# An attention kernel with bias: seven wide warm-up products for fourteen, the first two bias slots in a row, and the late k transposes behind score slot 2

## Chip, cores and metric

The kernel runs on one core of a Trainium2 chip. The metric is device time in microseconds (us) of one execution; lower is better. A timed run is mostly some 1.8 us longer than its span, because the span covers only the first to the last recorded instruction. Single runs of one kernel scatter by up to a microsecond, so that differences below 0.5 us need several runs each.

TensorE is PE in the views (its weight loads PEld), VectorE is DVE, ScalarE is ACT, GpSimd is POOL and SyncE is SP. PEq, SPq and ACTq are the queues of these engines. The columns of a timeline: start in us, duration in us, engine, line, operation, out<-in, count.

## The reference

```python
# batch 4, 8 heads, 1024 positions, 64 numbers per head; bias is 1 x 1 x 1024 x 1024
scores = (1.0 / np.sqrt(head_dim)) * np.matmul(q, k.transpose(0, 1, 3, 2)) + bias
scores_max = np.max(scores, axis=-1, keepdims=True)
attn = np.exp(scores - scores_max) / (np.sum(np.exp(scores - scores_max), axis=-1, keepdims=True) + 1e-8)
return np.matmul(attn, v).astype(np.float32)
```

## The kernel before

The kernel takes heads in 16 pairs. A score slot is up to three 128 x 512 products of k and q in PSUM; ACT exponentiates it (`s_exp`). exp(score + bias) is made as exp(score) times exp(bias), so the bias is exponentiated once, in four bias slots of 16 transposes and one ACT instruction each (`b_fill`, `b_exp`), and DVE multiplies it in. Two PSUM buffers (`ps_s`) serve score and bias slots in turn. After a hand-written opening, a small greedy scheduler, run when the program is built, puts the rest in order from estimated costs.

```python
    raws = {}
    trs = {}

    def load_qk(pr):
        qr = raw.tile([P, 2, NCH, D], BF, name="qr")
        kr = raw.tile([P, 2, NCH, D], BF, name="kr")
        nc.gpsimd.dma_start(out=kr.rearrange("p t c d -> p t (c d)"), in_=kf[pr])
        nc.gpsimd.dma_start(out=qr.rearrange("p t c d -> p t (c d)"), in_=qf[pr])
        raws[pr] = (qr, kr)
# ... cut ...
    def s_fill(g):
        if ("S", g) not in open_ps:
            open_ps[("S", g)] = ps_s.tile([P, 3, HQ], F32, tag="s", name="ps")
        ps = open_ps[("S", g)]
        for j, b in enumerate(slots[g]):
            pr, h, qh, kc = banks[b]
            qT, kT = trs[(pr, 0)], trs[(pr, 1)]
            nc.tensor.matmul(ps[:, j, :], kT[:, kc, :], qT[:, h, qh * HQ:(qh + 1) * HQ],
                             start=True, stop=b not in late_bias)
# ... cut ...
    def s_exp(g):
        n = len(slots[g])
        nc.scalar.activation(e_at(slots[g][0], n), open_ps.pop(("S", g))[:, :n, :], ACTF.Exp, scale=scale)

    def b_fill(qh, c0):

        ps = ps_s.tile([P, 3, 2 * HQ], BF, tag="s", name="pb").rearrange("p b (k c q) -> p (b k) c q", c=2, q=P)
        open_ps[("B", qh, c0)] = ps
        for c in range(2):
            for kc in range(NCH):
                nc.tensor.transpose(ps[:, kc, c, :],
                                    btraw[:, qh * QC + c0 + c, :].rearrange("p (kp kc) -> p kc kp", kc=NCH)[:, kc, :],
                                    ident[:])

    def b_exp(qh, c0):
        nc.scalar.activation(eb[:, qh, :, c0 * P:(c0 + 2) * P],
                             open_ps.pop(("B", qh, c0))[:, :NCH].rearrange("p k c q -> p k (c q)"), ACTF.Exp)
# ... cut: multiplication by exp(bias), products with v, division ...
        def evac():
            oh = small.tile([P, M, D], F32, name=f"oh{x}")
            rs = small.tile([P, M, 1], F32, name=f"rh{x}")
            nc.vector.reciprocal(rs[:], acc[:, :, D:D1])
            q = (nc.scalar, nc.sync)[x]
            if x == 0:
                for i in range(M):
                    nc.scalar.activation(oh[:, i, :], acc[:, i, :D], ACTF.Copy, scale=rs[:, i, :])
            else:
                nc.vector.tensor_tensor(oh[:], acc[:, :, :D], rs[:].to_broadcast([P, M, D]), op=ALU.mult)
            q.dma_start(out=of[2 * NP - 1][:, QC + x * M:QC + (x + 1) * M, :], in_=oh[:])
        return evac      # the last two stores of the kernel
```

The opening, which the change edits:

```python
        nc.gpsimd.dma_start(out=kr0[:, :, QC:, :].rearrange("p t c d -> p t (c d)"), in_=kf[0][:, :, QC * D:])
        nc.gpsimd.dma_start(out=btraw[:, :2, :], in_=bf_[:, :2, :])
        nc.gpsimd.dma_start(out=qr0[:, :, QC:, :].rearrange("p t c d -> p t (c d)"), in_=qf[0][:, :, QC * D:])
        nc.gpsimd.dma_start(out=btraw[:, 2:QC, :], in_=bf_[:, 2:QC, :])
        for x in range(2):
            for y in range(2):
                nc.vector.memset(mask[x * D:(x + 1) * D, y, :], 1.0 if x == y else 0.0)

        wm = ps_s.tile([P, 3, HQ], F32, tag="s", name="ps")
        open_ps[("S", 0)] = wm

        def dummy(n):
            nc.tensor.matmul(wm[:, 0, :n], zeros[:, :P], zeros[:, :n], start=True, stop=True)

        for i in range(12):
            dummy(HQ // 2)

        def k_trans(c0, n, tag):
            px = ps_x.tile([P, n, P], BF, tag=tag, name="px")
            for c in range(n):
                for t in range(2):
                    nc.tensor.transpose(px[t * D:(t + 1) * D, c, :], kr0[:, t, c0 + c, :], ident[:])
            return px
# ... cut: q_trans, q_out, first casts and copies ...
        q_out(1, pq1)
        nc.scalar.copy(kr0[:, :, 2:QC, :], k0f[:, :, 2:, :])
        dummy(P)
        dummy(P)
        s_fill(0)
        s_exp(0)
        s_fill(1)
        pk1 = k_trans(2, 2, "xa")
        nc.vector.tensor_copy(kT0[:, 2:QC, :], pk1[:])
        nc.vector.memset(vall[:, :, :, D:D1], 1.0)
        s_exp(1)
        pk2 = k_trans(QC, QC, "xb")
        s_fill(2)
        nc.vector.tensor_copy(kT0[:, QC:, :], pk2[:])
        s_exp(2)
        load_v(0)
        for c in (QC, QC + 2):
            nc.gpsimd.dma_start(out=btraw[:, c:c + 2, :], in_=bf_[:, c:c + 2, :])
        load_qk(1)
        load_v(1)
        load_qk(2)
        EXP, EXP0, QK, AV, TP = 427, 62, 216, 170, 350
        MUL, COPYQ, COPYK, EVAC, SEM = 600, 650, 420, 620, 80
        order = [("S", g) for g in range(3, NS)]
        for at, x in ((3, (0, 0)), (5, (0, 2)), (9, (1, 0)), (11, (1, 2))):
            order.insert(at, ("B",) + x)
        NO = len(order)
        T0 = 8000.0
        t_act, t_pe, t_dve = T0 + 1400, T0 + 200, T0 + 100
        filled = []
# ... cut: the scheduler ...
```

The softmax here doesn't subtract the row's maximum and nothing guards it: scores larger than these inputs give would overflow.

Of the kernel before, what the change touches and what calls it, by code (L numbers as in the profile page):

```python
# [9 lines left out]
BF = mybir.dt.bfloat16  # L10
# [5 lines left out]
def kernel(  # L16
# [15 lines left out]
    nc = tc.nc  # L32
    B, H, S, D = q.shape
    P = 128
# [4 lines left out]
    HQ = S // 2  # L39
    QC = NCH // 2  # L40
# [7 lines left out]
    consts = ctx.enter_context(tc.tile_pool(name="consts", bufs=1))  # L48
# [15 lines left out]

    k0f = consts.tile([P, 2, QC, D], F32)
    q0f = [consts.tile([P, QC, D], F32, name=f"q0f{t}") for t in range(2)]
    zeros = consts.tile([P, HQ // 2], BF)

    raws = {}
    trs = {}  # L70
# [8 lines left out]
    def load_v(pr):  # L79
        for t in range(2):  # L80
            nc.gpsimd.dma_start(out=vall[:, 2 * pr + t, :, :D], in_=vf[pr, :, t])  # L81
# [34 lines left out]
    def e_at(b, n):  # L116
        if b // ET not in etiles:
            etiles[b // ET] = ep.tile([P, ET, HQ], BF, name="E")
        return etiles[b // ET][:, b % ET:b % ET + n, :]
# [3 lines left out]
# [9 lines that stand above are left out]
            if b in late_bias:  # L132
                nc.tensor.matmul(ps[:, j, :], ident[:], braw[:, late_bias[b], :], start=False, stop=True)
# [4 lines that stand above are left out]
# [105 lines left out]
    with tc.manual_schedule():  # L243
# [12 lines left out]
        kT0 = kvp.tile([P, NCH, P], BF, name="kT")  # L256
# [13 lines left out]
        wm = ps_s.tile([P, 3, HQ], F32, tag="s", name="ps")  # L270
        open_ps[("S", 0)] = wm

        def dummy(n):
            nc.tensor.matmul(wm[:, 0, :n], zeros[:, :P], zeros[:, :n], start=True, stop=True)  # L274

        for i in range(12):
            dummy(HQ // 2)

        def k_trans(c0, n, tag):
            px = ps_x.tile([P, n, P], BF, tag=tag, name="px")  # L280
# [4 lines that stand above are left out]
# [18 lines left out]
            "p b (c q) -> p (b c) q", q=P)[:, :QC, :])  # L303
        q_out(1, pq1)
        nc.scalar.copy(kr0[:, :, 2:QC, :], k0f[:, :, 2:, :])
        dummy(P)
        dummy(P)
        s_fill(0)
        s_exp(0)
        s_fill(1)  # L310
# [1 line left out]
        nc.vector.tensor_copy(kT0[:, 2:QC, :], pk1[:])  # L312
        nc.vector.memset(vall[:, :, :, D:D1], 1.0)
        s_exp(1)
        pk2 = k_trans(QC, QC, "xb")
        s_fill(2)
        nc.vector.tensor_copy(kT0[:, QC:, :], pk2[:])  # L317
        s_exp(2)
        load_v(0)
        for c in (QC, QC + 2):  # L320
            nc.gpsimd.dma_start(out=btraw[:, c:c + 2, :], in_=bf_[:, c:c + 2, :])  # L321
# [7 lines left out]
        EXP, EXP0, QK, AV, TP = 427, 62, 216, 170, 350  # L329
        MUL, COPYQ, COPYK, EVAC, SEM = 600, 650, 420, 620, 80  # L330
        order = [("S", g) for g in range(3, NS)]
        for at, x in ((3, (0, 0)), (5, (0, 2)), (9, (1, 0)), (11, (1, 2))):
            order.insert(at, ("B",) + x)
        NO = len(order)
        T0 = 8000.0
        t_act, t_pe, t_dve = T0 + 1400, T0 + 200, T0 + 100
        filled = []
        act_end = []
        x_free = {"xa": T0 - 500, "xb": T0 + 100}
        x_unit = {}  # L340
        bias_at = {(0, 0): 10900, (0, 2): 13700, (1, 0): 18600, (1, 2): 20800}
        raw_at = {0: (5900, 11500), 1: (22200, 23500), 2: (26000, 28500)}
        pieces = [(0, 0, 1)]
        for pr in range(1, NP):
            pieces += [(pr, 1, 0), (pr, 0, 0), (pr, 1, 1), (pr, 0, 1)]

        pieces.append((NP, 0, 0))
        raw_at[NP] = (T0, T0)
        piece_end = {(0, 1, 0): T0, (0, 0, 0): T0, (0, 1, 1): T0 + 200}
        eb_at = {}  # L350
        exp_at = {x: T0 + (0 if x < 3 else 1400) for x in range(6)}
        mul_at = {}
# [16 lines left out]
        def pe_cost(t, c):  # L369
            return c * 2 if t < COLD else c  # L370
# [207 lines left out]
        while len(act_end) < NO or av_next < NA or any(last_left) or dve_q:  # L578
# [12 lines left out]
            if who == 0:  # L591
                i = a[2]
                item = order[i]
                t_act = t + a[1]
# [12 lines left out]
            elif who == 1:  # L607
                if d in dve_q:
                    dve_q.remove(d)
                t_dve = t + d[2]  # L610
                d[3](t)
            else:
                t_pe = t + pe_cost(t, p[1])
# [31 lines left out]
```

## Time and profile before

| | before |
|---|---|
| device time, median of 3 (lowest to highest) | 249.80 us (249.74 to 250.32) |
| span of the profiled run | 249.0 us |
| ACT busy | 240.1 us, 96% |
| start of the unbroken run of 161 exponentials | 27.53 us |
| its 161 exponentials | 215.95 us |
| start of ACT's last store issue | 244.87 us |
| from there to the end of the span | 4.13 us |

The span of this kernel can be read as three stretches, which I shall call **front**, **middle** and **tail**. The front ends where ACT's unbroken run begins. The middle reaches from there to the start of ACT's last store issue: 244.87 - 27.53 = 217.34 us. The tail is the rest: 249.0 - 244.87 = 4.13 us. It holds the landing of the last two stores and the closing of the program.

The page has the whole span's count of these blocks:

```profile
q8 instruction: 25, 0.41, 0.7%
```

0.41 MB / 25 is some 16 KB each. The Trainium skill's page "Runtime: NRT & Kernel Launch", section "Instruction fetch mechanics", says that an engine's instruction memory is refilled in blocks of 16 KiB, 256 instructions, by the engine's own DMA queue while it executes, and that the cost of crossing a block boundary is "mostly hidden". The size agrees, and 25 x 256 = 6400 is near the 6354 instructions of PE in the built program (DVE, the next, has 419), so I take q8 for PE's.

### The profile page before, as it was taken

What the parts mean: (1) busy time and instruction counts of PE and PEld (TensorE: products, weight loads), DVE (VectorE), ACT (ScalarE), POOL (GpSimd) and SP (SyncE); (2) the same over time, 40 slices, a digit from 0 to 9 for tenths busy, and PEclk for the clock granted to TensorE, in tenths of its full rate; (3) what the DMA queues carried; (4) which work ended last, traced back from release to release, by engine and by line L of the source; (5) the groups of instructions that cost most, each with busy time, mean ns of one, the idle gap of its engine ahead of it and who ended that gap; (6) DMA issues with size and microseconds to landing.
All of it is one profiled execution on the core that took longest, in us unless ns stands there. A gap on an engine that the chain in (4) does not pass through costs nothing.

```text
span 249.0 us, 7149 instructions
## 1 busy us (share of the span) xinstructions
PE 226.3 (91%) x3106; PEld 141.6 (57%) x3160; DVE 219.0 (88%) x381; ACT 240.1 (96%) x183; POOL 54.6 (22%) x76
## 2 busy tenths in 40 slices
PE   8768999999999999999999999999999999998892
PEld 4335656556665665665656555666555555565561
DVE  5207899999999999999999999999998999999883
ACT  5999999999999999999999999999999999999991
POOL 6654534202213501303230041416000000000000
PEclk9999999999999999999999999999999999999999
DMA  5999999923925994922992049789901101020201
GB/s 118 176 199 192 202 135 197 98 84 45 147 56 100 135 81 121 90 88 29 180 133 84 5 95 118 94 124 122 131 3 42 46 23 65 3 84 3 87 32 57
DMA packets 48752, 23.80 MB, mean 96 GB/s; under 512 B 34512, under 2 KB 44624, under 8 KB 48720
## 3 DMA queue, kind: packets, MB, share of 16 engines
q0 software_dynamic: 42560, 14.42, 53.5%
q1 hardware_dynamic: 5872, 8.72, 9.7%
q8 instruction: 25, 0.41, 0.7%
q10 hardware_dynamic: 288, 0.20, 0.3%
q14 instruction: 7, 0.06, 0.1%
HBM read 29.36 MB, written 8.39 MB: 152 GB/s over the span
## 4 chain that ended last, share of the span: by engine, by line
ACT 65%; PE 18%; DVE 7%; DMA 5%; issue 2%; POOL 1%; ACTq 0%
ACT E L137 64%; PE ps L130 11%; DMA kr<-in_k_dram 5%; PE po L188 3%; DVE E L163 2%; PE px L89 2%; PE ps L274 1%; DVE E L160 1%; DVE E L157 1%; DVE oall L200 1%; DVE qT L98 1%; ACT eb L150 1%; POOL vall L81 1%; POOL btraw L321 0%; PE pb L145 0%
## 5 line engine op out<-in xcount | busy, mean ns | idle before, releaser
L137 ACT ACTIVATE E<-ps 128x1536 bf16<-128x1536 f32 (+2 forms) x172 | 230.1, 1666 | 0.7 <-PE ps L130 0.7
L130 PE MATMUL ps<-qT,kT 128*128 128x512 bf16 x458 | 134.8, 379 | 12.1 <-ACT E L137 5.6
L188 PEld LDWEIGHTS <-E 128*128 128x128 bf16 x2016 | 82.0, 98 | 40.2 <-DVE E L160 3.8
L160 DVE TENSOR_TENSOR E<-E,eb 128x2048 bf16<-128x2048 bf16 x78 | 93.9, 1216 | 5.9 <-ACT eb L150 5.7
L188 PE MATMUL po<-vall,E 128*128 128x65 bf16 x2016 | 92.7, 194 | 2.5 <-DVE E L160 1.3
L130 PEld LDWEIGHTS <-kT 128*128 128x128 bf16 x512 | 45.1, 97 | 41.6 <-issue 9.9
L163 DVE TENSOR_TENSOR E<-E,eb 128x1024 bf16<-128x1024 bf16 x92 | 61.1, 684 | 1.9 <-ACT E L137 1.4
L75 POOL DMA_DIRECT2D kr<-in_k_dram x15 | 10.5, 699 | 87.1 <-PE px L89 84.1
L81 POOL DMA_DIRECT2D vall<-in_v_dram x32 | 28.1, 883 | 4.8 <-DVE kT L317 3.5
L200 DVE TENSOR_TENSOR oall<-po,rs 128x256 f32<-128x256 f32 x63 | 26.7, 425 | 2.2
L98 DVE TENSOR_TENSOR qT<-px,mask 128x1024 bf16<-128x1024 bf16 x31 | 21.3, 688 | 6.7 <-PE px L89 6.0
L76 POOL DMA_DIRECT2D qr<-in_q_dram x15 | 10.7, 715 | 26.0 <-PE px L89 22.8
L102 DVE COPY kT<-px 128x512 bf16<-128x512 bf16 x30 | 12.6, 421 | 1.9 <-PE px L89 1.5
L198 DVE RECIPROCAL rs<-po 128x4 f32<-128x4 f32 x63 | 11.1, 177 | 2.4 <-PE po L188 2.2
L89 PE MATMUL px<-ident,kr 128*64 128x128 bf16 x240 | 12.4, 224 | 0.8 <-DMA kr<-in_k_dram 0.6
L89 PE MATMUL px<-ident,qr 128*64 128x128 bf16 x248 | 12.8, 225 | 0.1
L89 PEld LDWEIGHTS <-qr 128*64 128x64 bf16 x248 | 7.9, 109 | 8.0 <-issue 5.1
L89 PEld LDWEIGHTS <-kr 128*64 128x64 bf16 x240 | 7.7, 109 | 7.6 <-issue 4.5
L150 ACT ACTIVATE eb<-pb 128x2048 bf16<-128x2048 bf16 x4 | 7.5, 1883 | 0.4 <-PE pb L145 0.4
L145 PE MATMUL pb<-ident,btraw 128*128 128x128 bf16 x64 | 4.6, 225 | 1.2 <-ACT eb L150 1.0
L145 PEld LDWEIGHTS <-btraw 128*128 128x128 bf16 x64 | 4.4, 146 | 1.5 <-issue 1.1
L157 DVE TENSOR_TENSOR E<-E,eb 128x1024 bf16<-128x1024 bf16 (+2 forms) x7 | 4.6, 686 | 0.2 <-ACT E L137 0.2
(45 smaller groups left out, 28.2 us busy)
## 6 DMA issues: line engine op xcount, KB each, us to landing
out_dram<-oall SPq DMA_DIRECT2D x28, 256.0 KB, 2.0
vall<-in_v_dram POOLq DMA_DIRECT2D x32, 128.0 KB, 5.9
kr<-in_k_dram POOLq DMA_DIRECT2D x15, 256.0 KB, 4.5
qr<-in_q_dram POOLq DMA_DIRECT2D x15, 256.0 KB, 5.2
btraw<-in_bias_dram POOLq DMA_DIRECT2D x4, 512.0 KB, 8.5
out_dram<-oall SPq DMA_DIRECT2D x7, 128.0 KB, 3.5
k0f<-in_k_dram SPq DMA_DIRECT2D x2, 128.0 KB, 3.0
q0f<-in_q_dram ACTq DMA_DIRECT2D x1, 128.0 KB, 2.5
```

The source lines that it names most:

```text
L76: nc.gpsimd.dma_start(out=qr.rearrange("p t c d -> p t (c d)"), in_=qf[pr])
L81: nc.gpsimd.dma_start(out=vall[:, 2 * pr + t, :, :D], in_=vf[pr, :, t])
L89: nc.tensor.transpose(px[t * D:(t + 1) * D, c, :], src[:, t, half * QC + c, :], ident[:])
L98: nc.vector.tensor_tensor(dst[:, :, half * HQ:(half + 1) * HQ], px.rearrange("p c q -> p (c q)").unsqueeze(1).to_broadcast([P, 2, HQ]), ma ...
L102: nc.vector.tensor_copy(dst[:, half * QC:(half + 1) * QC, :], px[:])
L130: nc.tensor.matmul(ps[:, j, :], kT[:, kc, :], qT[:, h, qh * HQ:(qh + 1) * HQ], start=True, stop=b not in late_bias)
L137: nc.scalar.activation(e_at(slots[g][0], n), open_ps.pop(("S", g))[:, :n, :], ACTF.Exp, scale=scale)
L160: nc.vector.tensor_tensor(e, e, eb[:, qh, kc:kc + 2, :].unsqueeze(2).to_broadcast([P, 2, 2, HQ]), op=ALU.mult)
L163: nc.vector.tensor_tensor(e, e, eb[:, qh, kc:kc + 1, :].to_broadcast([P, n, HQ]), op=ALU.mult)
L188: nc.tensor.matmul(acc[:, i, :], e[:, 0, i * P:(i + 1) * P], vall[:, 2 * pr + h, kc, :], start=(kc == 0 and i == 0), stop=(kc == NCH - 1), ...
L198: nc.vector.reciprocal(rs[:], acc[:, :, D:D1])
L200: nc.vector.tensor_tensor(oall[:, c0:c0 + QC, :], acc[:, :, :D], rs[:].to_broadcast([P, QC, D]), op=ALU.mult)
```

## The change

The intent is a cheaper opening. (1) TensorE is warmed by seven dummy products of the same total width in place of fourteen, over a smaller tile of zeros. (2) The eight late k transposes leave the path to score slot 2. (3) The first two bias slots are taken in a row, ahead of the transposes of the second half of q, so that exp(bias) for the first half of the queries is ready sooner. The other edits are the scheduler's estimates for the new order.

```diff
--- before.py
+++ after.py
@@ -64,7 +64,7 @@
 
     k0f = consts.tile([P, 2, QC, D], F32)
     q0f = [consts.tile([P, QC, D], F32, name=f"q0f{t}") for t in range(2)]
-    zeros = consts.tile([P, HQ // 2], BF)
+    zeros = consts.tile([P, P], BF)
 
     raws = {}
     trs = {}
@@ -271,10 +271,11 @@
         open_ps[("S", 0)] = wm
 
         def dummy(n):
-            nc.tensor.matmul(wm[:, 0, :n], zeros[:, :P], zeros[:, :n], start=True, stop=True)
-
-        for i in range(12):
-            dummy(HQ // 2)
+            nc.tensor.matmul(wm[:, 0, :n * P], zeros[:, :P], zeros[:, :P].unsqueeze(1).to_broadcast([P, n, P]),
+                             start=True, stop=True)
+
+        for i in range(6):
+            dummy(QC)
 
         def k_trans(c0, n, tag):
             px = ps_x.tile([P, n, P], BF, tag=tag, name="px")
@@ -303,8 +304,7 @@
             "p b (c q) -> p (b c) q", q=P)[:, :QC, :])
         q_out(1, pq1)
         nc.scalar.copy(kr0[:, :, 2:QC, :], k0f[:, :, 2:, :])
-        dummy(P)
-        dummy(P)
+        dummy(2)
         s_fill(0)
         s_exp(0)
         s_fill(1)
@@ -312,10 +312,11 @@
         nc.vector.tensor_copy(kT0[:, 2:QC, :], pk1[:])
         nc.vector.memset(vall[:, :, :, D:D1], 1.0)
         s_exp(1)
+        s_fill(2)
+        s_exp(2)
         pk2 = k_trans(QC, QC, "xb")
-        s_fill(2)
-        nc.vector.tensor_copy(kT0[:, QC:, :], pk2[:])
-        s_exp(2)
+        nc.vector.tensor_copy(kT0[:, QC:QC + 1, :], pk2[:, :1, :])
+        nc.vector.tensor_copy(kT0[:, QC + 1:, :], pk2[:, 1:, :])
         load_v(0)
         for c in (QC, QC + 2):
             nc.gpsimd.dma_start(out=btraw[:, c:c + 2, :], in_=bf_[:, c:c + 2, :])
@@ -329,24 +330,24 @@
         EXP, EXP0, QK, AV, TP = 427, 62, 216, 170, 350
         MUL, COPYQ, COPYK, EVAC, SEM = 600, 650, 420, 620, 80
         order = [("S", g) for g in range(3, NS)]
-        for at, x in ((3, (0, 0)), (5, (0, 2)), (9, (1, 0)), (11, (1, 2))):
+        for at, x in ((3, (0, 0)), (4, (0, 2)), (9, (1, 0)), (11, (1, 2))):
             order.insert(at, ("B",) + x)
         NO = len(order)
         T0 = 8000.0
-        t_act, t_pe, t_dve = T0 + 1400, T0 + 200, T0 + 100
+        t_act, t_pe, t_dve = T0 + 1400, T0 + 200, T0 + 600
         filled = []
         act_end = []
-        x_free = {"xa": T0 - 500, "xb": T0 + 100}
+        x_free = {"xa": T0 - 500, "xb": T0 + 600}
         x_unit = {}
         bias_at = {(0, 0): 10900, (0, 2): 13700, (1, 0): 18600, (1, 2): 20800}
-        raw_at = {0: (5900, 11500), 1: (22200, 23500), 2: (26000, 28500)}
+        raw_at = {0: (5900, 14300), 1: (22200, 23500), 2: (26000, 28500)}
         pieces = [(0, 0, 1)]
         for pr in range(1, NP):
             pieces += [(pr, 1, 0), (pr, 0, 0), (pr, 1, 1), (pr, 0, 1)]
 
         pieces.append((NP, 0, 0))
         raw_at[NP] = (T0, T0)
-        piece_end = {(0, 1, 0): T0, (0, 0, 0): T0, (0, 1, 1): T0 + 200}
+        piece_end = {(0, 1, 0): T0, (0, 0, 0): T0, (0, 1, 1): T0 + 500}
         eb_at = {}
         exp_at = {x: T0 + (0 if x < 3 else 1400) for x in range(6)}
         mul_at = {}
```

## The prediction

> **What bounds the kernel now.** I read the page first (busy shares), then the waits of ScalarE (ACT), then ACT's timeline, and last the chain of waits of the first 30 us, because every part of the change sits in the first 28 us. The page's first section and the waits of ACT:
>
> ```profile
> PE 226.3 (91%) x3106; PEld 141.6 (57%) x3160; DVE 219.0 (88%) x381; ACT 240.1 (96%) x183; POOL 54.6 (22%) x76
> ```
>
> ```profile
> ACT oh L237 <- DVE rh L233: 0.8, 1, 0.8
> ACT E L137 <- PE ps L130: 0.7, 3, 0.2
> ...
> ACT eb L150 <- PE pb L145: 0.4, 1, 0.4
> ```
>
> ACT computes 172 exponentials of scores (L137) and 4 of the bias (L150) and is busy 240.1 of 249.0 us. After the first score exponential starts (5.71 us) it waits only 0.23 + 0.25 + 0.21 us ahead of its first three exponentials, 0.36 us ahead of the fourth bias slot, and 0.84 us in the tail. ACT's timeline:
>
> ```profile
> 23.94 1.45 ACT L137 ACTIVATE E<-ps 128x1536 bf16<-128x1536 f32 x1
> 25.75 1.88 ACT L150 ACTIVATE eb<-pb 128x2048 bf16<-128x2048 bf16 x1 [0.36 <-PE pb L145]
> 27.53 215.95 ACT L137 ACTIVATE E<-ps 128x1536 bf16<-128x1536 f32 x161
> ```
>
> From 27.53 to 243.48 us ACT never stops: 161 exponentials, 215.95/161 = 1.341 us each. The change alters no size or number there, so the end moves by as much as the start of that unbroken run moves, which is set by the fourth bias exponential at 25.75. What released that one? The chain of waits, first 30 us (start, us, what):
>
> ```profile
> 8.53 1.75 POOL vall L81 x2
> 10.28 1.06 POOL btraw L321 x2
> 11.34 11.35 DMA kr<-in_k_dram
> 22.69 0.04 issue
> 22.73 0.41 PE px L89 x8
> ...
> 24.72 1.01 PE pb L145 x16
> 25.73 0.02 issue
> 25.75 1.88 ACT eb L150
> 27.63 2.69 ACT E L137 x2
> ```
>
> So the path does not come from ACT's early work. It comes from the load of the next pair's k, issued at 11.34 and landed at 22.69. TensorE (PE), in order, stands at the 8 transposes that need it; then come one score slot (3 matmuls), some AV matmuls (scores times v), 8 q transposes and the 16 bias transposes, and only then can ACT go on. ACT had run without a gap from 7.78 until here.
>
> **What the Trainium skill says.** "TensorE: Matmul & The Clock Gate", section "Back-to-back issue gap", gives N/1.2 ns from matmul to matmul while cold. The 12 dummies of 256 columns took 2.74 us with 0.421 us for one: (2.74 - 0.421)/11 = 0.211 us, and 256/1.2 = 0.213. The trace agrees. The same page, "What's actually happening", has the clock go full after a busy window of about 3.4 us that is free-running. In the trace a 512-column matmul takes 0.61 us at 5.06 us and 0.39 us at 6.90, so the switch lies between; whether it is free-running one trace can't show. "ScalarE: Activation LUTs", section "What ACT_TABLE_LOAD costs", gives 186 ns + 0.833 ns per element with 93 ns of overlap: 1.373 us a step for 1536 elements, where the trace has 1.341; I use the trace. "Perfetto Trace Analysis", section "Per-instruction lifecycle", says that the slice of a DMA issued by GpSimd ends when the descriptors are written, not when data has moved. The trace agrees: the k load's slice is 0.71 us, its landing 11.35 us after the issue.
>
> **The change part by part.**
>
> (1) Dummies. Twelve of 256 columns become six of 512; two of 128 become one of 256. Columns before: 12 x 256 + 2 x 128 = 3328; after: 6 x 512 + 256 = 3328. Cold spacing goes with columns, so PE is busy equally long: 11 x 0.211 + 0.421 = 2.74 us before; after, 5 x 0.422 + 0.61 = 2.72 us. The memset of the zeros is halved, 0.17 us to some 0.1 (an estimate by size), so they may start 0.07 us earlier. The first transposes wait for q anyway: its cast ends at 3.28 + 0.29 = 3.57. Worth 0 to 0.07 us at the first exponential.
>
> (2) Eight late k transposes behind score slot 2. Before, they stand ahead of slot 2: 8 of about 0.04 us, 0.3 us. Slot 2's second matmul, however, reads a k copy that DVE finishes at 6.79 + 0.29 = 7.08, and that weight load went at 7.13. The first matmul had started at 6.90, so the transposes hid under this copy. Slot 2 should end near 7.7 either way: gain 0 to 0.1 of the 0.21 us wait. The copy of these 8 chunks becomes one of 128 columns and one of 384. By 0.29 us for 256 columns (L312) and 0.42 for 512 (L102) they cost about 0.23 + 0.36 = 0.59 us; the next slot needs only the short one, at about 8.4, while ACT is busy with slot 2 until 9.2.
>
> (3) Bias slots in a row. The built order shows ACT doing score slots 3 to 5, bias, bias, slot 6, where it was bias, slot 6, bias. The second bias half is late:
>
> ```profile
> 13.84 0.14 PEld L145 LDWEIGHTS <-btraw 128*128 128x128 bf16 x1 [0.21 <-DMA btraw<-in_bias_dram]
> ```
>
> From about 13.8, 16 transposes last 1.15 us (as the same group at 15.08 did): ready at about 15.0. The first bias exponential ends at 13.13 + 1.90 = 15.03. It fits with nothing to spare. The q transposes now follow at about 14.85; their DVE copy (0.69 us) ends near 16.0; slot 6 is ready at about 16.7, before ACT is through with the second bias at 16.9. Both bias exponentials are done 1.2 us earlier, so DVE starts its multiplications at about 17.0 in place of 18.18:
>
> ```profile
> 18.18 4.63 DVE L160 TENSOR_TENSOR E<-E,eb 128x2048 bf16<-128x2048 bf16 x4 [5.67 <-ACT eb L150]
> ```
>
> But only four of them (4.63 us) can go before the other half of the bias is exponentiated at about 27.6. DVE will simply stand idle later, from about 21.6 to 23.2. Worth nothing by itself.
>
> (4) What the earlier products do to PE's order around the path. In the built order after the change, between slot 10 and the fourth bias slot stand 4 + 24 AV matmuls; before, 8 AV, 8 q transposes and 4 AV. Before, AV began at 23.74 and the bias transposes at 24.55: 0.81 us. After: a run of 20 AV took 0.79 us with 0.193 for one, so (0.79 - 0.193)/19 = 0.0314 us each; 28 x 0.0314 = 0.88 us. **That is 0.07 us more on the path.** The q transposes move behind the bias group, where the next slot has about 0.4 us to spare.
>
> Sum: parts 1 to 3 give 0 to 0.2 us before the gate at 22.69, which swallows it; part 4 costs 0.07 us behind it; the tail's order on ACT, DVE and PE is the same. Net 249.8 + 0.07 = 249.9 us.
>
> **The rivals.** *The k load lands earlier or later.* It is queued behind the v and bias loads, whose issue waits for a DVE memset at about 8.2 to 8.5. If the new DVE order frees that memset earlier and the queue isn't already full, all landings move forward by some tenths. Against it: the memset stands at the same place in DVE's order, and the DMA share is above 1.0 from 8 us on, so queued bytes set the landing. The wait of 0.36 us could vanish at most: 249.4 us. If it lands 0.4 us later: 250.3 us. *A stall at the second bias slot takes over.* If its load lands after 13.9, ACT waits there. But the fourth bias slot has 0.36 us of PE wait in hand, so up to that much is hidden; half a microsecond more late gives 250.0 us. *The early start does carry through*, if the landing is not the gate on most runs: all three early waits (0.69 us) are then partly recovered, at most 249.2 us. *The new greedy order opens a stall later.* DVE is busy 31.2 of 32 us in 28 to 60; but ACT didn't wait on it once in 216 us, so I give this little.
>
> **Range and chances.** The three runs before span 249.74 to 250.32, so 0.6 us is noise of a run. Landing time and warm-up add about 0.3 us either way. Range 249.2 to 250.5. A change of over 2% is 5 us, seven times all early waits together: faster 0.01, slower 0.01, same 0.98.
>
> **What would show it.** Right: six dummies end near 3.7 us and the first exponential is at 5.6 to 5.75; slot 2's exponential at 7.6 to 7.8; two bias exponentials in a row from about 13.1 with under 0.15 us between; DVE's first multiplication near 17.0 and then an idle stretch before 23; the k load landing at 22.5 to 22.9 and the fourth bias exponential at 25.7 to 25.9 after a wait of 0.3 to 0.6 us; 161 exponentials without a gap. Wrong: a landing that moved by over 0.3 us, a fourth bias exponential without a wait, or waits of ACT on DVE after 28 us.

## More of the kernel before

The timeline of the last stores of the kernel before (columns: start in us, duration in us, engine, line, operation, out<-in, count):

```profile
244.83 1.12 SPq L240 DMA_DIRECT2D out_dram<-oh  x1
244.87 0.36 ACTq L240 DMA_DIRECT2D out_dram<-oh  x1
```

The DMA view of the same kernel from 244 to 249 us (queues: packets, MB, share of the 16 engines; issues: KB each, median us from issue to landing):

```profile
q8 instruction: 1, 0.02, 1.2%
...
out_dram<-oh SPq DMA_DIRECT2D x1, 64.0 KB, 2.3
out_dram<-oh ACTq DMA_DIRECT2D x1, 64.0 KB, 2.0
```

Two stores of 64 KB end the work, and they land 2.3 and 2.0 us after their issue. In the same stretch the queue q8 brings one block of the program's instructions; narrower windows put it between 244 and 245 us.

## The result, and the profile after

| | before | after |
|---|---|---|
| median of 6 runs of the same rounds | 250.18 us | 249.37 us |
| lowest to highest | 249.74 to 250.75 | 249.05 to 249.89 |
| ratio of the runs, after over before | | 0.9966, 95% interval 0.9947 to 0.9985 |
| span of the profiled run | 249.0 us | 247.3 us |
| front (start of the unbroken run) | 27.53 us | 26.66 us |
| middle | 217.34 us | 217.35 us |
| tail | 4.13 us | 3.29 us |

A ratio is the mean time of one kernel's runs over the mean of the other's runs of the same rounds, so it is not quite the ratio of the medians beside it. The change takes 0.8 us away (250.18 - 249.37), a third of a per cent: within 2%, and inside the predicted range, but downward where the prediction had 0.07 us upward.

The page of the kernel after, first section:

```profile
PE 230.0 (93%) x3153; PEld 140.3 (57%) x3153; DVE 218.7 (88%) x379; ACT 239.9 (97%) x183; POOL 54.8 (22%) x76
```

Against the line in the prediction, weight loads fell from 3160 to 3153: the seven products that are gone. (The count of matmuls in a trace is not to be used so; records can be missing.) ACT is as busy as before. Its timeline after:

```profile
7.38 5.48 ACT L137 ACTIVATE E<-ps 128x1536 bf16<-128x1536 f32 x4 [0.18 <-PE ps L130]
12.75 3.67 ACT L150 ACTIVATE eb<-pb 128x2048 bf16<-128x2048 bf16 x2
...
23.45 1.46 ACT L137 ACTIVATE E<-ps 128x1536 bf16<-128x1536 f32 x1
24.89 1.88 ACT L150 ACTIVATE eb<-pb 128x2048 bf16<-128x2048 bf16 x1
...
26.66 215.95 ACT L137 ACTIVATE E<-ps 128x1536 bf16<-128x1536 f32 x161
```

The two bias exponentials now stand in one group of two, and the fourth bias exponential (24.89) has lost its wait of 0.36 us. The unbroken run starts at 26.66 in place of 27.53, 0.87 us sooner: 0.40 of it is already there at score slot 2 (7.38 in place of 7.78), 0.36 is the vanished wait, and the remaining 0.1 is spread over gaps too short to be named. The chain of waits of the kernel after agrees; its first 30 us contain no DMA piece any more, where before the k load stood for 11.35 us:

```profile
7.38 5.48 ACT E L137 x4
...
26.77 4.03 ACT E L137 x3
```

The tail changed as well. The timeline of the last stores after:

```profile
243.96 0.34 SPq L240 DMA_DIRECT2D out_dram<-oh  x1
244.01 0.36 ACTq L240 DMA_DIRECT2D out_dram<-oh  x1
```

And the DMA view of the kernel after from 243 us to the end, with all its queues:

```profile
q1 hardware_dynamic: 288, 0.20, 14.3%
q10 hardware_dynamic: 144, 0.07, 4.9%
q14 instruction: 1, 0.01, 0.6%
...
out_dram<-oh SPq DMA_DIRECT2D x1, 64.0 KB, 1.6
```

There is no block on q8 in it, the page counts 24 where it counted 25, SyncE's issue took 0.34 us in place of 1.12, and its store landed after 1.6 us in place of 2.3. Before, that store landed at 244.83 + 2.3 = 247.1, and the span ended 1.9 us later; after, at 243.96 + 1.6 = 245.6, and the span ended 1.7 us later. So 0.7 of the 0.84 us that the tail lost is the faster landing.

The two profiles thus differ by 0.87 us in the front and 0.84 in the tail, 1.7 us in all, but the medians of the timed runs differ by 0.8. One of the two must be the luck of the profiled run. The experiments had to find which, and which part of the change the other belongs to.

### The profile page after: what moved, and what is told of

Its sections match the earlier page's. It is cut to its first block, busy times and chain, and to the rows that moved or that the text cites. A ratio compares the mean times of both kernels' runs of the same rounds, so it can differ in the third digit from the quotient of the medians. Undisturbed runs are those within 1.5% of the kernel's fastest.

```text
span 247.3 us, 7186 instructions
## 1 busy us (share of the span) xinstructions
PE 230.0 (93%) x3153; PEld 140.3 (57%) x3153; DVE 218.7 (88%) x379; ACT 239.9 (97%) x183; POOL 54.8 (22%) x76
## 4 chain that ended last, share of the span: by engine, by line
ACT 73%; PE 15%; DVE 8%; issue 2%; ACTq 0%
ACT E L137 70%; PE ps L130 9%; ACT eb L150 3%; DVE E L163 3%; PE po L188 3%; PE ps L274 1%; DVE oall L200 1%; DVE E L160 1%; DVE E L157 1%; PE px L89 1%; DVE qT L98 1%; DVE rs L198 0%; DVE kT L102 0%; PE px L289 0%; PE px L284 0%
## 5 line engine op out<-in xcount | busy, mean ns | idle before, releaser
L130 PE MATMUL ps<-qT,kT 128*128 128x512 bf16 x512 | 138.9, 378 | 9.0 <-ACT E L137 5.3
L160 DVE TENSOR_TENSOR E<-E,eb 128x2048 bf16<-128x2048 bf16 x81 | 97.6, 1216 | 1.3 <-ACT eb L150 0.9
L163 DVE TENSOR_TENSOR E<-E,eb 128x1024 bf16<-128x1024 bf16 x86 | 57.0, 684 | 2.2 <-ACT E L137 1.4
```

Source lines behind the costliest of these rows:

```text
L160: nc.vector.tensor_tensor(e, e, eb[:, qh, kc:kc + 2, :].unsqueeze(2).to_broadcast([P, 2, 2, HQ]), op=ALU.mult)
L163: nc.vector.tensor_tensor(e, e, eb[:, qh, kc:kc + 1, :].to_broadcast([P, n, HQ]), op=ALU.mult)
```

## The experiments

Twelve kernels ran, four to a chip, with its own runs of the kernel before (medians 250.51, 250.26 and 250.36 us), 6 runs each beside 11 of the kernel before. All gave correct results. For each profiled run, front + 217.35 us + tail gives the span to 0.1 us, so the table carries all of it. "Last q8 block" is the window of one microsecond in which the last block of instructions was recorded between 236 us and the end of the record. "Slot 2" is the start of its exponential.

| run | what it is | median us | ratio to before (95%) | slot 2 | front | tail | last store's landing | last q8 block |
|---|---|---|---|---|---|---|---|---|
| before | | | 1 | 7.78 | 27.53 | 4.13 | 2.3 | 244 |
| after | parts 1+2+3 | 249.37 | 0.9966 (0.9947 to 0.9985) | 7.38 | 26.66 | 3.29 | 1.6 | none |
| e1 | part 1 | 249.86 | 0.9984 (0.9958 to 1.0010) | 7.96 | 27.64 | 3.32 | 1.6 | none |
| e2 | part 2 | 250.28 | 1.0000 (0.9978 to 1.0023) | 8.01 | 27.19 | 3.96 | 2.2 | 244 |
| e3 | part 3 | 250.98 | 1.0022 (0.9995 to 1.0050) | 8.10 | 27.31 | 4.54 | 2.8 | 244 |
| e4 | before, one memset early | 250.24 | 0.9992 (0.9972 to 1.0012) | 7.58 | 27.03 | 4.13 | 2.4 | 244 |
| e5 | after again | 249.69 | 0.9981 (0.9966 to 0.9996) | 7.98 | 27.16 | 3.29 | 1.6 | none |
| e6 | parts 2+3 | 250.30 | 1.0007 (0.9988 to 1.0026) | 7.24 | 28.27 | 4.19 | 2.5 | 245 |
| e7 | after + 14 instructions | 250.62 | 1.0004 (0.9988 to 1.0021) | 7.21 | 27.56 | 4.30 | 2.6 | 245 |
| e8 | parts 1+2 | 249.52 | 0.9964 (0.9949 to 0.9979) | 8.01 | 27.20 | 3.36 | 1.6 | none |
| e9 | parts 1+3 | 249.31 | 0.9962 (0.9938 to 0.9987) | 7.70 | 26.87 | 3.28 | 1.6 | 248 |
| e10 | after + 80 instructions | 249.48 | 0.9975 (0.9946 to 1.0005) | 7.48 | 27.21 | 3.35 | 1.6 | 241 |
| e11 | parts 1+2, one memset early | 250.16 | 0.9995 (0.9967 to 1.0024) | 7.67 | 28.05 | 3.31 | 1.6 | none |
| e12 | parts 1+2 again | 249.87 | 0.9988 (0.9952 to 1.0023) | 7.11 | 27.54 | 3.32 | 1.6 | 249 |

The front scatters from 26.7 to 28.3 us with no order by part of the change (with part 3, 27.29 us in the mean of seven traces; without it, 27.45). The tail falls into two groups with a gap between them: 3.28 to 3.36 us, and 3.96 to 4.54 us.

### e1: the wide dummies alone

```diff
-    zeros = consts.tile([P, HQ // 2], BF)
+    zeros = consts.tile([P, P], BF)
-            nc.tensor.matmul(wm[:, 0, :n], zeros[:, :P], zeros[:, :n], start=True, stop=True)
-        for i in range(12):
-            dummy(HQ // 2)
+            nc.tensor.matmul(wm[:, 0, :n * P], zeros[:, :P], zeros[:, :P].unsqueeze(1).to_broadcast([P, n, P]),
+                             start=True, stop=True)
+        for i in range(6):
+            dummy(QC)
-        dummy(P)
-        dummy(P)
+        dummy(2)
```

> The kernel before with part 1 alone (wide dummies, halved zeros). Theory W: the wide dummies themselves bring the full clock sooner; the third score matmul (start near 5.9 us) is then already fast (0.39 us in place of 0.61), the first k transposes start near 6.05 in place of 6.45, and the kernel gains some 0.4 us or more of the 0.8. Rival F: the switch falls by chance (free-running); then this kernel is within 0.1 us of before in the timed runs, whatever its one trace shows.

Ratio 0.9984. The front was no sooner (27.64 us, against 27.53), yet the tail was 3.32 us. One line of the DMA view from 244 to 249 us, the last store's landing:

```profile
out_dram<-oh SPq DMA_DIRECT2D x1, 64.0 KB, 1.6
```

So the short tail comes with part 1 alone, which edits nothing behind 5 us. The interval of the ratio reaches to 1.001, and by itself it shows no gain. The record also has the span of every run, and there the gain is clear: 247.98 us in the mean of the six runs, against 248.69 of the eleven of the kernel before, a difference of 0.71 us with a 95% interval (Welch's) of 0.16 to 1.26. The trace holds a second thing. The timeline of this run, with the k transposes still ahead of slot 2:

```profile
6.75 0.41 PE L284 MATMUL px<-ident,kr 128*64 128x128 bf16 x8 [0.28 <-DMA kr<-in_k_dram]
...
7.96 1.45 ACT L137 ACTIVATE E<-ps 128x1536 bf16<-128x1536 f32 x1 [0.59 <-PE ps L130]
```

PE waited for the late half of k and ACT behind it for 0.59 us. In this run PE was fast early (its first three score products took 0.94 us, against 1.45 before), so the load became the later of the two.

### e2: the late k transposes behind slot 2, alone

```diff
-        pk2 = k_trans(QC, QC, "xb")
         s_fill(2)
-        nc.vector.tensor_copy(kT0[:, QC:, :], pk2[:])
         s_exp(2)
+        pk2 = k_trans(QC, QC, "xb")
+        nc.vector.tensor_copy(kT0[:, QC:QC + 1, :], pk2[:, :1, :])
+        nc.vector.tensor_copy(kT0[:, QC + 1:, :], pk2[:, 1:, :])
# and three start estimates of the scheduler
```

> The kernel before with part 2 alone (late k transposes behind slot 2, copy split). Theory: slot 2 is held by the copy of the first k chunks and not by the transposes, so the third score exponential stays at 7.7 to 7.8 us and the time within 0.1 us of before. Rival: the eight transposes were on the path; exponential 0.2 to 0.3 us sooner, time 0.2 to 0.3 us less.

Ratio 1.0000, tail 3.96 us, 25 blocks on q8. Slot 2 stood at 8.01 us, later than either theory had it. Part 2 alone moves nothing that the runs can see.

### e3: the two bias slots in a row, alone

```diff
-        for at, x in ((3, (0, 0)), (5, (0, 2)), (9, (1, 0)), (11, (1, 2))):
+        for at, x in ((3, (0, 0)), (4, (0, 2)), (9, (1, 0)), (11, (1, 2))):
-        raw_at = {0: (5900, 11500), 1: (22200, 23500), 2: (26000, 28500)}
+        raw_at = {0: (5900, 14300), 1: (22200, 23500), 2: (26000, 28500)}
```

> The kernel before with part 3 alone (first two bias slots in a row). Theory on record: nothing by itself, and 0.07 us more between slot 10 and the fourth bias slot through 28 AV matmuls; time 0 to 0.1 us more than before. Rival: the q transposes, moved off, free the fourth bias slot of its wait of 0.36 us; time 0.3 us less.

Ratio 1.0022, interval 0.9995 to 1.0050; tail 4.54 us. Part 3 alone brings nothing, and may cost some tenths of a microsecond.

### e4: the kernel before, with the memset of v's ones ahead of everything

This tests what sets the landing of the next pair's k, which the prediction called the gate. GpSimd's loads wait for a DVE memset of v's last column. If the time of issue is the gate (theory G in the expectation), an early memset moves the landing forward; if the bytes queued ahead are (Q), it doesn't.

```diff
-        for x in range(2):
+        nc.vector.memset(vall[:, :, :, D:D1], 1.0)
+        def mask_rows(x):
             for y in range(2):
                 nc.vector.memset(mask[x * D:(x + 1) * D, y, :], 1.0 if x == y else 0.0)
+        mask_rows(0)
 # ... cut ...
         q_out(1, pq1)
+        mask_rows(1)
 # ... cut ...
-        nc.vector.memset(vall[:, :, :, D:D1], 1.0)
```

> The kernel before with the memset of v's ones column moved to the head of DVE's list (two of the four mask memsets move later to make room). Theory G: the k load is gated by this memset (it ends 1.15 us after the first k copy, then v, bias and k loads are issued in turn), so the v loads are issued near 5.1 us in place of 8.5, the k load near 7.9 in place of 11.3, it lands 0.8 to 3 us sooner, the fourth bias exponential has no wait, time 0.3 to 0.5 us less. Rival Q, as the prediction had it: queued bytes set the landing; it stays at 22.4 to 22.9 us and the time within 0.1 us.

Ratio 0.9992. The timeline of POOL in this run, the issue of that k load:

```profile
7.87 0.71 POOL L75 DMA_DIRECT2D kr<-in_k_dram  x1
```

The issue came 3.5 us sooner (11.34 before), but the landing only 0.8 us: the DMA view gives 14.0 us from issue to landing, so 21.9 us, against 22.69. That is at the edge of what G had (0.8 to 3 us sooner), and in this trace the wait at the fourth bias slot is gone, as G had it; but the timed runs show no gain of 0.3 us (interval 0.9972 to 1.0012). Other traces settle it: e11, below, has the same early issue and a landing at 23.2 us, the latest of all, while e8 and e9, issued after 11.2 us, landed at 21.2 and 20.9. So the time of issue doesn't set the landing, and G falls. That the queued bytes do, no run tests by itself. The run cost something too: the first bias slot waited 0.17 us, as the second half of q landed about 0.4 us later than before.

### e5 and e6: the kernel after once more, and with its part 1 undone

e5 is the kernel after, unchanged, to see which features of its trace come back. e6 is parts 2 and 3 on the kernel before, that is, the kernel after with the dummy lines of e1 undone.

```diff
 # e6 against the kernel after: the lines of e1 the other way round
-        for i in range(6):
-            dummy(QC)
+        for i in range(12):
+            dummy(HQ // 2)
 # ... and the other three places ...
```

> The changed kernel itself, on the chip of the next three, as their anchor. All theories: some 0.3% below before (249.3 to 249.9 us), 24 instruction loads of queue 8, none of them after 243 us, tail (issue of ACT's last store to the end of the span) near 3.3 us.

> The changed kernel with part 1 undone (12 + 2 narrow dummies, equal columns, 14 PE instructions more). Theory I: the 15 fewer PE instructions keep the 25th instruction load of 16 KB out of the last microseconds, where it delays the last stores; here it returns (25 loads, one after 243 us), the last SyncE store takes 1.0 to 1.6 us in place of 0.33, tail 4.0 to 4.5 us, time 0.6 to 1.0 us more than e5. Theory W: wide dummies bring the clock sooner; the tail stays 3.3 us and the third score exponential starts 0.3 to 0.5 us later.

e5 repeats the gain (0.9981, interval below 1) and the tail (3.29 us). It does not repeat the early front: slot 2 stood at 7.98 us and the unbroken run at 27.16. The 0.40 us at slot 2 in the first trace of the kernel after were the luck of that run. The first three score products of PE show what the luck is. In the kernel before's timeline:

```profile
5.06 1.45 PE L130 MATMUL ps<-qT,kT 128*128 128x512 bf16 x3
```

in the first trace of the kernel after:

```profile
5.01 1.10 PE L130 MATMUL ps<-qT,kT 128*128 128x512 bf16 x3
```

in e5, the same kernel:

```profile
5.31 1.41 PE L130 MATMUL ps<-qT,kT 128*128 128x512 bf16 x3
```

and in e6, with the narrow dummies:

```profile
5.00 0.97 PE L130 MATMUL ps<-qT,kT 128*128 128x512 bf16 x3
```

Wide dummies gave 1.10 and 1.41 us, narrow ones 1.45 and 0.97. PE becomes fast at a different moment from run to run, and the width of the dummies alone does not decide it. Over all 14 traces the three products took 1.1 us or less in seven of nine with wide dummies and in two of five with narrow ones, too few to say whether width shifts the odds. The prediction cited the page "TensorE: Matmul & The Clock Gate", section "What's actually happening", which has this moment vary by some 500 ns because the clock's window is free-running. The runs agree that it varies; why, they do not show.

e6 loses the gain: 1.0007, tail 4.19 us, a q8 block between 245 and 246 us. Everything else of the change is still in it. Its DMA view from 244 to 249 us:

```profile
q8 instruction: 1, 0.02, 1.4%
...
out_dram<-oh SPq DMA_DIRECT2D x1, 64.0 KB, 2.5
```

Its front was the latest of all, 28.27 us, and its waits of ACT say why:

```profile
ACT eb L150 <- PE pb L145: 1.4, 1, 1.4
```

PE was fast early, ACT reached the second bias slot soon, and the bias had not landed until 13.9 us. This is the prediction's rival "a stall at the second bias slot": here it follows an early start. In this trace the early start was worth nothing; it ran into a load that had not landed.

### e7: the kernel after with seven surplus transposes

Part 1 does two things: its dummies are wide, and its program has fewer PE instructions (counted in the built programs, 6354 before, 6340 with part 1 alone and 6339 after; the fifteenth, a semaphore instruction, goes with part 3). e7 keeps the wide dummies and puts 14 instructions back elsewhere, which makes 6353, as in e6: seven transposes, each with its weight load, into an unused column of the second bias slot.

```diff
         open_ps[("B", qh, c0)] = ps
+        if (qh, c0) == (0, 2):
+            for i in range(7):
+                nc.tensor.transpose(ps[:, NCH, 0, :], btraw[:, 0, :P], ident[:])
```

> The changed kernel with 7 surplus transposes (14 PE instructions, results never read) in the gap in which PE waits for the second bias load; dummies stay wide. Theory I: the 25th instruction load returns, tail 4.0 to 4.5 us, time 0.6 to 1.0 us more than e5 though not one dummy changed. Theory W: 7 short transposes in a wait cost nothing, time within 0.15 us of e5.

The gain is gone: 1.0004. The DMA view of e7 from 243 to 250 us:

```profile
q8 instruction: 1, 0.02, 0.9%
...
out_dram<-oh SPq DMA_DIRECT2D x1, 64.0 KB, 2.6
out_dram<-oh ACTq DMA_DIRECT2D x1, 64.0 KB, 2.7
```

The q8 block is back (245 to 246 us), the stores land 1.0 us later than after, and the tail is 4.30 us, 1.0 us longer. So the width of the dummies is not what makes the tail short; the number of PE instructions is what e1, e6 and e7 have in common. One reservation: ACT also waited 1.0 us at bias slots in this trace, so the ratio alone would not tell the two apart; the tail does. SyncE's issue, at 0.33 us, was short here though the landing was late, so the long issue slice of the kernel before (1.12 us) is not the necessary part of it.

### e8: parts 1 and 2, the bias order undone

```diff
 # the kernel before with the edits of e1 and e2; those of e3 are left out
```

> The changed kernel with part 3 undone (bias slots apart, q transposes between). The prediction's step 4: 0.07 us less on the path at the fourth bias slot, which is to say nothing; the runs with part 2 or part 3 alone had no wait there. Theory: within 0.2 us of e5, tail 3.3 us. Rival: the row of bias slots is worth a part of the 0.8 us, time 0.3 us or more above e5.

0.9964, tail 3.36 us: as good as the kernel after on the same chip (e5, 0.9981), with overlapping intervals. The bias order brings nothing that can be seen.

### e9: parts 1 and 3, the late k undone

```diff
 # the kernel before with the edits of e1 and e3; those of e2 are left out
```

> The changed kernel with part 2 undone (eight late k transposes again ahead of slot 2). Tail 3.3 us as in every kernel with 24 instruction loads, so 0.5 to 0.8 us below before. Theory: part 2 is worth something only where the clock rises early, as then the late half of k lands after PE is ready for it (6.4 to 6.8 us); on average 0 to 0.2 us above the changed kernel's ratio of 0.997 to 0.998. Rival: part 2 is what carries the gain; ratio to before 0.9995 or more.

0.9962, tail 3.28 us. Part 2 brings nothing that can be seen either. The DMA view of this run holds a detail for one microsecond after the span had ended at 247.5, from 248 to 249 us:

```profile
q8 instruction: 1, 0.02, 5.6%
```

Here the 25th block was recorded after all, only later (the page, which ends with the span, counts 24): the stores had landed at about 245.8. e12 shows one at 249 us. In the other short tails none is recorded.

### e10: the kernel after with 80 more PE instructions in its middle

If the number of blocks made the tail long, 80 more instructions should make it long again. If the place of the last block does (theory P), the load should move forward, away from the stores, and the tail should stay short.

```diff
             qT, kT = trs[(pr, 0)], trs[(pr, 1)]
+            if j == 0 and 40 <= g < 80:
+                nc.tensor.matmul(ps[:, 0, :32], kT[:, kc, :], qT[:, h, qh * HQ:qh * HQ + 32], start=True, stop=True)
```

> The changed kernel with 40 surplus short matmuls (80 PE instructions, overwritten at once by the real ones) in score slots 40 to 79, the middle of the kernel. Theory P, place: the 25th instruction load is back but falls 75 or so PE instructions before the end, at 242 to 243.5 us, ahead of the last stores; tail 3.3 to 3.5 us and time as the changed kernel (ratio to before 0.997 to 0.9985). Rival N, number: whatever loads 25 blocks pays for the 25th; tail 4.0 to 4.5 us and ratio 0.9995 or more.

The page counts 25 blocks again; the last one stands in the DMA view from 240 to 242 us:

```profile
q8 instruction: 1, 0.02, 4.9%
```

and in that from 243 to 248 us the store is as fast as after:

```profile
out_dram<-oh SPq DMA_DIRECT2D x1, 64.0 KB, 1.6
```

Tail 3.35 us with 25 blocks: the place counts, not the number. The ratio, 0.9975 with an interval to 1.0005, points the same way without being proof by itself. The block fell at the early edge of what I had expected (242 to 243.5 us): a narrower window, 241.9 to 242.0, has its start. An estimate from the kernel before fits: its last two blocks are some 10 us apart (234 and 244 us), 256 instructions in between, 26 per us; e10 has 6419 instructions, 65 more than the kernel before, 65 / 26 = 2.5 us ahead of 244.6, where the block of the kernel before starts, so 242.1.

### e11 and e12: two combinations without the bias order

e11 is parts 1 and 2 with the early memset of e4; e12 is parts 1 and 2 once more, as e8, on the third chip. They look for a version that beats both kernels.

```diff
 # e11: the edits of e1, e2 and e4 on the kernel before
 # e12: the edits of e1 and e2 on the kernel before
```

> Parts 1 and 2 without part 3, and the early memset: a candidate for the fastest. If the landing of the k load follows queued bytes (as e4 showed: issued 3.5 us sooner, landed 0.1 to 0.6 us sooner), the memset adds nothing: within 0.15 us of e12, or 0.1 to 0.2 us worse through the q half that lands later. If it does take the wait at the fourth bias slot away in the runs with an early clock: 0.1 to 0.3 us less than e12.

> Parts 1 and 2 without part 3, as e8, on this chip: ratio to before 0.996 to 0.998, tail 3.3 us, 24 instruction loads; at or a little below the changed kernel.

0.9995 and 0.9988, both intervals across 1, both tails short (3.31 and 3.32 us). Their fronts were late, 28.05 and 27.54 us, with waits of ACT at bias slots (0.8 us in e12). The early memset adds nothing, and no version stands clear of the kernel after. In spans both lie below the kernel before of the same rounds (247.92 and 247.77 us against 248.45); the part on what was wrong comes back to this.

## Why the prediction was right and where it was wrong

**The range held, the direction and the cause did not.** The step that failed is "the end moves by as much as the start of that unbroken run moves", which the sum closes with "the tail's order on ACT, DVE and PE is the same". The order is the same, and the middle is the same to 0.01 us. But what follows the last instruction of the engines, the landing of the last stores, is not a constant: it takes 1.6 or 2.2 to 2.8 us, according to whether a block of instructions is loaded beside it. That the range held is owed to its width of 1.3 us. One of its rivals even names 249.4 us, from a k load that lands sooner and takes away the wait of 0.36 us; the load did so in the profiled run, but e1 (landing at 22.8 us, short tail) and e2 (21.4 us, no gain) show that the gain doesn't come from there, so that agreement is luck.

**The mis-sized term is part 1.** It was valued by its columns at 0 to 0.07 us, at the first exponential. Its columns are indeed worth that: the six dummies took 2.74 us in the chain of waits, predicted 2.72, and the first exponential stood at 5.68 us against 5.71. What it was not valued for are its 14 fewer PE instructions. In the kernels with 6353 or 6354 of them the last block of 256 is loaded beside the last stores; in those with 6339 or 6340 behind the stores or not at all within the record. The eight profiled kernels without a block among their last stores have tails of 3.28 to 3.36 us, mean 3.32; the six with one have 3.96 to 4.54, mean 4.21, a difference of 0.9 us. The timed runs, by other means, agree in size: the mean of the ratios of the eight is 0.9977 and that of the five with a block (e2, e3, e4, e6, e7) 1.0005, a difference of 0.28%, or 0.7 us of 250. Shown by runs are the tie to part 1 (e1, e6), to the number of instructions and not to the width (e7), and to the place of the load (e10).

**A part of the gain is lost again after the span.** By spans, seven kernels with the short tail (all but the kernel after itself, whose rounds have no recorded spans of the kernel before) lie 0.74 us below the kernel before of their rounds and the five with a block 0.08 us above it: 0.82 us between them, near the 0.9 us of the tails, where the times give 0.65. The rest stands behind the last recorded instruction. The time of a run less its span is over 2.0 us in 13 of the 48 runs of the eight kernels (up to 3.01 us, in e12) and in 1 of the 63 runs of the others (2.37 us). That the block, moved there, holds up the end of these runs is likely, since e12's trace has it at 249 us, behind its span; it is not shown.

**Why one block delays the stores.** The DMA engines are far from full in that time (in the kernel before from 244 to 249 us, 12.7% + 4.4% + 1.2% + 0.4% for the four queues, 19% in all), but an average over 16 engines hides one that is taken. The block is one packet; 1.2% of 16 engines in 5 us is 1.0 us of one engine, from 244.6 to some 245.6. The last two stores of SyncE are 144 packets each on q1. In the kernel after the first of them passes at once, here in the DMA view from 244.1 to 244.75 us:

```profile
q1 hardware_dynamic: 144, 0.13, 64.4%
```

In the kernel before, 135 of the 144 pass from 245.0 to 245.55 us, and the last nine only from 245.55 to 246.3, when the block is through (DMA views of these two windows). SyncE's second store follows behind them, from 246.4 to 246.8 us.

```profile
q1 hardware_dynamic: 135, 0.12, 65.5%
...
q1 hardware_dynamic: 9, 0.01, 6.2%
```

135 is 15/16 of 144, and 6.2% is one engine of 16. So the part of a store that falls to the engine of the block seems to stand behind it. In all six traces with a block among the last stores, the last nine or so packets of one of SyncE's two stores come in this way; in none of the others do those stores show it. The trace names no engine for a packet, so the reading is drawn from these counts.

**What stays open.** The runs do not show what moved the block in the kernel after from 244 us to 248 or later for 15 instructions. A plausible reading is that PE has run dry by then, so that the count which asks for the block is reached only in the closing instructions; that is argued, not shown.

**Part 2** was predicted at 0 to 0.1 us ahead of the gate and nothing behind it; e2 (1.0000) and e9 agree. The reason given, that the transposes hide under the wait for a k copy, holds where the clock rises late. The prediction did not see that with an early clock the old order waits for the late half of k itself (0.28 us on PE in e1).

**Part 3** was predicted at nothing: DVE starts sooner and stands idle later. It did: multiplications from 16.45 us in place of 18.18, then an idle stretch of 1.3 us ahead of the next k copy. The rival of the stall at the second bias slot appeared under the new bias order in e6 (1.42 us), e7 (0.75 us) and e10 (0.45 us), where slot 2 stood at 7.24, 7.21 and 7.48 us, but not in after (7.38), e5, e9 or e3: in after the bias load landed at 13.3 us, in those three at 13.9. The prediction reckoned with half a microsecond for it.

**Part 4**, 0.07 us more on the path through the 28 products ahead of the fourth bias slot, stood in the built order as predicted, but that path no longer set the time in this trace: the k load landed about 0.8 us sooner (21.9 us in place of 22.69), outside the predicted 22.5 to 22.9, and ACT found the fourth bias slot ready. The wait of 0.36 us comes and goes from run to run (0.38 in e1 and e12, none in e2, e3, e5, with and without the change). "The gate swallows an early start" was right in kind: slot 2 stood anywhere from 7.11 to 8.10 us and the unbroken run did not follow it. e12 with 7.11 reached 27.54, e8 with 8.01 reached 27.20. What swallows it is sometimes the k load, sometimes a bias load.

**The signs that were promised.** Right: the dummies' end, the first exponential, two bias exponentials back to back (at 12.75 us, predicted 13.1), DVE's early start (16.45, predicted 17.0) and later idle time, 161 exponentials without a gap. Wrong: slot 2 (7.38), the landing, and the fourth bias exponential without a wait. The prediction had named the last two as signs of being wrong, and they were real in that trace; e1, with a landing at 22.8 us and a wait of 0.38 us, has the short tail all the same, and e2, e3 and e4, without that wait, have no clear gain, so they were not the cause of the 0.8 us.

## What to carry to other kernels

When a profile's end moves more than any engine's work explains, split the span at the first and the last instruction of the bounding engine, compare the pieces over several profiles, and look at the DMA queues in the last microseconds, the instruction queue included. Instructions that cost no time where they stand can still decide when the next block of 256 is loaded; in this kernel 14 or 15 instructions more or fewer were worth about 0.7 us, and with 80 cheap ones added in the middle the tail was as short as with 15 taken away. It is a small, fragile gain: an edit that changes the number of instructions can lose it again, as e7 did. And an average share of the DMA engines can look low while the one engine that a store still needs is taken.

## What the Trainium skill lacked or had wrong

- "Runtime: NRT & Kernel Launch", section "Instruction fetch mechanics", calls the cost of a block boundary "mostly hidden". Through the middle of this kernel that agrees (front to tail took 217.35 us to 0.1 us in every trace, whatever the blocks). Among the last stores it does not: tails of 3.96 to 4.54 us with a block there, 3.28 to 3.36 without. The page has nothing on a load that competes with a kernel's last stores.
- No page that I read tells of the wait ahead of the DVE memset of v's ones, 128 x 256 elements with a large stride: the trace of the kernel after records 0.27 us, but ahead of it an idle time of 0.89 us that is put down to issue (0.88 us in e10). Whether the memset itself holds DVE so long no run tested.
